# Weight splits run further ahead, adding DMAs issued earlier, the sum over the conv tiles on VectorE

## The chip, the cores and the metric

The kernel runs on one core of a Trainium2 chip. The metric is device time in microseconds (us) of one execution. PE is TensorE, DVE is VectorE, ACT is ScalarE, POOL is GpSimd, and SP is the engine whose queue issues the weight loads.

## What is computed

One layer of a decoder trunk on 256 tokens of width 1024, in float32:

```
n = RMSNorm(x)
z = n @ w_in                      # a, gate, q, k, v, qi, ki, wi, gc, ga from one projection
u = a * sigmoid(gate)
u = causal depthwise conv of u, 31 taps, per channel, + conv_b
y_conv = silu(layernorm(u) over the channels) @ w_conv_out
y_attn = attention over the 64 keys that an indexer picks, @ w_attn_out
h = x + (sigmoid(gc) * y_conv + sigmoid(ga) * y_attn) @ w_mix_out
h = h + CrossAttn(RMSNorm(h), RMSNorm(mem))       # 4 heads, 256 memory tokens
h = h + W2 relu(W1 RMSNorm(h))^2                  # 1024 -> 4096 -> 1024
return RMSNorm(h)
```

## The kernel before

**Weights.** All weights come as 83 chunks of 128x2048 float32 (1 MB each) in the order in which the products need them: conv, qi, ki, gc, ga, v, q and k, xk and xv (cross attention on the memory), ao (attention out), co (conv out), mix, xq, xo, then f1 and f2 in turn. SP loads a chunk into one of three `raw` buffers. To keep float32 precision each operand is used as a high part plus a low part, and a product takes three matmuls (high by high, high by low, low by high). So each chunk is split in two halves of 128x1024. `high()` (L185) lets ACT copy a half into a rounded `hi` tile (L189) and queues a job `low()`, which lets DVE subtract, raw - hi (L198), into a `lo` tile. For ten of the halves (the second half of every third chunk from the ninth chunk to the first of ao) it is done otherwise: ACT writes lo = -hi (L192), and `low()` has GpSimd issue a DMA that adds raw onto lo (L196). After the low of a chunk's last half, `low()` issues the load of the next chunk into the raw buffer that came free. There are six `hi` and six `lo` buffers (`HALVES`), reused in turn.

**How far ahead.** `weights()` hands a half to its user and counts it in `nused`; `nsplit` counts the halves whose high has been issued. `split_high()` issues the next high only while `nsplit - nused < HALVES - held`. `held` is 1, and is 2 where two halves are in use at once. `split_ahead()` (L230) issues one low, unless a chain has `waiting` set, and then one high. It is called once after each `weights()`.

**Order.** The order of the instructions on each engine is that in which the program issues them; the framework adds the semaphores. A tile of a result buffer that is given a new owner is written only when all instructions that use the old contents have been done. Each product goes over half chunks: `form_b` (L291) takes a half chunk, calls `split_ahead()`, runs a 128-column tile over all eight k tiles, hands the result to `after` and calls `tick()`. `form_b_late` (L302) does the same for two tiles together, with the last k tile of both left to the end, so that the operand can come late; it sets `held` to 2 for its length. It is used for the first chunk of co, mix, xq and f1 (co 0 is the first). The xo products work by k instead: `form_c` (L907) takes one half for all eight output tiles, and `form_c_last` (L917) takes both halves of the last xo chunk, and runs pairs of output tiles through both, each pair followed by `xo_residual` (L938): a DVE add into h_t, two ACT copies to the high part of `ff_p`, and one pair later two DVE instructions for its low part. f1 begins with `ff_p`.

**Fill.** The conv's 240 tap instructions on DVE (8 tiles by 30; the first tap of each tile is on ACT) are filler: `tick()` (L235) advances all pending chains by a step, and then issues taps while DVE's account stands more than 1000 below PE's. Both accounts are sums of prices in ns of what was issued on a counted engine (`pe` and `dve`, L62 to L108; a DVE instruction costs columns/0.96 plus 70, or plus 125 with a per-partition scalar). Whatever is issued through `nc.vector` or `nc.gpsimd` directly isn't counted. A finished conv tile goes into `done`; from the second on, GpSimd adds it onto `usum` (L475, 256 columns, seven times). When the eighth is finished, the chain `layer_norm` (L623) is started, before the last of these adds is issued. Its steps, one per `tick()`: one that only allocates; the mean from `usum` by a matmul (`ps_mub`) with four DVE subtractions, ACT squares and DVE adds, after which `waiting` is set until the next step, so that the next `split_ahead()` issues no low; then the variance, and the scaling and silu of four pairs of tiles into `u_p`, the operand of co. This runs during the ao products, whose results pass through DVE too (`ya`, `ga_t`, two instructions each). `gated` (L748) makes co's result into `mix_p`: ACT copies half of the bank to `yc`, DVE adds the other half, multiplies by the gate and adds (`gc_t`), ACT makes the high part of `mix_p`, and DVE the low part of the tile before.

Of the kernel before, what the change touches and what calls it, by code (L numbers as in the profile page):

```python
# [8 lines left out]
F32 = mybir.dt.float32  # L9
# [3 lines left out]
ALU = mybir.AluOpType  # L13
# [98 lines left out]
def block_kernel(ctx, tc, x, xt, mem, memt, wst, wki, vecs, convw, gout, out):  # L112
    nc = tc.nc
    ctx.enter_context(tc.manual_schedule())
    pe = Counted(nc.tensor, pe_price)
    dve = Counted(nc.vector, dve_price)
# [11 lines left out]
    def t8(name, dt=F32, shape=(P, KT, S)):  # L128
        return big.tile(list(shape), dt, tag="t8", bufs=12, name=name)
# [31 lines left out]
    def load(parts=1):  # L161
        if nload[0] >= len(STREAM):
            return
        c = nload[0]
        nload[0] += 1
        key = STREAM[c]
        raw = t8(f"raw{c}", F32, (P, N_CHUNK)) if c in EARLY else raws.tile([P, N_CHUNK], F32, tag="raw", name=f"raw{c}")
        n = KT * NK if key[0] == "ki" else N_CHUNK
        src = wki if key[0] == "ki" else wst[INDEX[key]]
        for q in range(parts):  # L170
            ns = slice(q * n // parts, (q + 1) * n // parts)
            nc.sync.dma_start(raw[:, ns], src[:, ns])
        if key in WHOLE:
            whole[key] = raw.rearrange("p (k n) -> p k n", k=2 * KT)
            return
        parts = 1 if key[0] == "ki" else 2
        for q in range(parts):
            ns = slice(q * n // parts, (q + 1) * n // parts)
            high_jobs.append(lambda ns=ns, q=q, last=q == parts - 1: high(key, c, raw, ns, q, last))

    def low_by_dma(key, c, q):

        return q == 1 and c % 3 == 2 and 8 <= c < STREAM.index(("ao", 1))

    def high(key, c, raw, ns, q, last):  # L185
        n = ns.stop - ns.start
        hi = highs.tile([P, N_CHUNK // 2], F32R, tag="hi", name=f"hi{c}_{q}")[:, :n]
        lo = lows.tile([P, N_CHUNK // 2], F32R, tag="lo", name=f"lo{c}_{q}")[:, :n]
        act(hi, raw[:, ns], AF.Copy)  # L189
        by_dma = low_by_dma(key, c, q)  # L190
        if by_dma:
            act(lo, hi.bitcast(F32), AF.Copy, scale=-1.0)  # L192

        def low():
            if by_dma:
                nc.gpsimd.dma_start(lo.bitcast(F32), raw[:, ns], accum_op=ALU.add)  # L196
            else:
                dve.tensor_tensor(out=lo, in0=raw[:, ns], in1=hi.bitcast(F32), op=ALU.subtract)  # L198
            prepared[(*key, q)] = (hi, lo)
            if last and c not in EARLY:  # L200
                load()

        low_jobs.append(low)

    def split_high():
        if high_jobs and nsplit[0] - nused[0] < HALVES - held[0]:
            nsplit[0] += 1
            high_jobs.pop(0)()

    def split_low():  # L210
        if low_jobs:
            low_jobs.pop(0)()

    nsplit, nused, held = [0], [0], [1]

    def weights(kind, i, half, kt):

        key = (kind, i, half)
        while key not in prepared:
            split_high()  # L220
            split_low()
        nused[0] += 1
        return [w.rearrange("p (k n) -> p k n", k=kt) for w in prepared.pop(key)]


    chains, fill, turn, done = [], [], [0], []
# [3 lines left out]
    def split_ahead():  # L230
        if not waiting[0]:
            split_low()
        split_high()

    def tick():  # L235
        for c in list(chains):
            if next(c, "end") == "end":
                chains.remove(c)
        while (len(fill) > 1 or (fill and (len(done) > 5 or nused[0] < 5))) and dve.total < pe.total - 1000:
            fill_one()  # L240
        dve.total = max(dve.total, pe.total - 2000)
# [14 lines left out]
    def start(gen):  # L256
        chains.append(gen)
        return gen
# [10 lines left out]
    def mm_b(ps, wh, wl, x2, kt, start, stop):  # L269
        mm3(ps, wh, wl, x2.high(kt), x2.low(kt), start, stop)  # L270
# [20 lines left out]
    def form_b(kind, i, x2, after, ps_of=ps_mm):  # L291

        for ct in range(2):
            w = weights(kind, i, ct, KT)
            split_ahead()
            ps = ps_of(f"ps_{kind}{i}{ct}")
            wide = is_wide(kind, 2 * i + ct)
            tile_b(ps, w, x2, wide=wide)
            after(2 * i + ct, ps if wide else ps[:, :S])
            tick()  # L300
# [158 lines left out]
    acc = t8("acc")  # L459
    usum = cst.tile([P, S], F32, tag="sums", bufs=2, name="usum")  # L460

    def tap(t, s):
        def go():
            j = TAPS - 1 - s
            if s == 0:
                act(acc[:, t, :], u[:, t, :], AF.Identity, scale=cw[:, t, j : j + 1], bias=cvb[:, t : t + 1])
            else:
                dve.scalar_tensor_tensor(out=acc[:, t, s:], in0=u[:, t, : S - s], scalar=cw[:, t, j : j + 1],
                                         in1=acc[:, t, s:], op0=ALU.mult, op1=ALU.add)
            if s == TAPS - 1:  # L470
                done.append(t)
                if len(done) == KT:
                    norms.append(start(layer_norm()))
                if len(done) > 1:
                    nc.gpsimd.tensor_tensor(out=usum, in0=usum if len(done) > 2 else acc[:, done[0], :],  # L475
                                            in1=acc[:, t, :], op=ALU.add)
        return go

    def conv_tile(i, half):
        key = ("conv", i)  # L480
        w = weights("conv", i, half, KT) if key not in WHOLE else None
        split_ahead()
        ps = ps_mm(f"ps_conv{i}{half}")
        if w:
            tile_b(ps, w, n2)
        else:
            for kt in range(KT):
                pe.matmul(ps[:, :S], whole[key][:, half * KT + kt, :], n_f[:, kt, :], start=kt == 0, stop=kt == KT - 1)
        return ps
# [132 lines left out]
    def layer_norm():  # L622
        u2.append(parts_t8("u_p"))  # L623
        yield
        mub = ps_aux("ps_mub")[:, :S]
        pe.matmul(mub, onesd, usum, start=True, stop=True)
        mub = mub.unsqueeze(1).to_broadcast([P, 2, S])
        vs = w2("vs", F32, (P, 2, S))
        pairs = [slice(2 * c, 2 * c + 2) for c in range(4)]
        for c, cs in enumerate(pairs):  # L630
            dve.tensor_tensor(out=acc[:, cs, :], in0=acc[:, cs, :], in1=mub, op=ALU.subtract)
            sq = vs if c == 0 else w2(f"sq_vr{c}", F32, (P, 2, S))
            act(sq, acc[:, cs, :], AF.Square)
            if c > 1:
                dve.tensor_tensor(out=vs, in0=vs, in1=before, op=ALU.add)
            before = sq
        waiting[0] = True
        yield
        waiting[0] = False
        dve.tensor_tensor(out=vs, in0=vs, in1=before, op=ALU.add)  # L640
        dve.tensor_tensor(out=vs[:, 0, :], in0=vs[:, 0, :], in1=vs[:, 1, :], op=ALU.add)
        yield
        rs = rsqrt(vs[:, 0, :], "vr")
        yield
        while len(headed) < NH:
            yield
        act(table, table, AF.Silu)
        rsb = spread(rs, "rsb").unsqueeze(1).to_broadcast([P, 2, S])
        for c in range(5):
            if c < 4:  # L650
                dve.tensor_tensor(out=acc[:, pairs[c], :], in0=acc[:, pairs[c], :], in1=rsb, op=ALU.mult)
                for t in (2 * c, 2 * c + 1):
                    act(acc[:, t, :], acc[:, t, :], AF.Silu, scale=lng[:, t : t + 1], bias=lnb[:, t : t + 1])
            if c > 0:
                parts_of(2 * c - 2)
            yield
# [260 lines left out]

    def form_c_last(kind, i, dst, x2, ks, after):
        w = [weights(kind, i, k, 1) for k in range(2)]
        held[0] = 2  # L920
        for ct in range(0, KT, 2):
            for k in range(2):
                for t in (ct, ct + 1):
                    cs = slice(t * P, t * P + P)
                    mm_b(dst[t], w[k][0][:, 0, cs], w[k][1][:, 0, cs], x2, ks + k, False, k == 1 and t % 2 == 1)
            after(ct)
            if ct % 4 == 2:
                tick()
        held[0] = 1
# [8 lines left out]
    def xo_residual(ct):  # L938
# [12 lines left out]
        lows_of.append(low)  # L951

    form_c_last("xo", 1, dst, ox2, 2, xo_residual)
    lows_of.pop()()

# [196 lines left out]
```

## Time and profile before

| | us |
|---|---|
| median of 3 runs (lowest, highest) | 516.12 (515.67, 516.19) |
| the profiled execution | 516.69 |
| its span, from the first to the last instruction | 514.9 |
| outside of the span | 1.8 |

The granted TensorE clock of the profiled execution is 0.998 of full speed over the span. The whole working below is made against the profiled execution. In the views a row gives the start in us, the length in us, the engine, the line, the operation, output<-input with the tiles' names, and in brackets the idle time of the engine ahead of it and who ended it. Instructions issued through the two counted engines all carry line 77, so they are told apart by the tiles' names.

### The profile page before, as it was taken

Reading aid. Unit: us, or ns where it says so; the run is one execution under the profiler, and the core shown is the slowest. Engines: PE = TensorE matmul, PEld = TensorE weight load, DVE = VectorE, ACT = ScalarE, POOL = GpSimd, SP = SyncE. Lnnn points to the kernel's source line nnn. Section 1 sums busy time; section 2 is a strip of 40 time slices with the busy share of each in tenths; the row PEclk is TensorE's granted clock in tenths of the full one; section 3 lists DMA queues with packets and bytes.
Section 4 is the critical chain, followed back from the end, with each engine's and each line's share of the span. In section 5 each row is a group of like instructions: output and inputs, shape, how many; then the busy total and the mean of one; then the engine's idle time right before and its main releaser. Section 6 shows DMA issues by size and latency. Waiting matters only on the chain.

```text
span 514.9 us, 8076 instructions
## 1 busy us (share of the span) xinstructions
PE 503.6 (98%) x3098; PEld 448.6 (87%) x3098; DVE 421.6 (82%) x822; ACT 305.3 (59%) x523; POOL 27.8 (5%) x40
## 2 busy tenths in 40 slices
PE   8999999999999999999999999999999999999995
PEld 6999998888899999888788998988888888888884
DVE  4998999999988999999989976796766566666565
ACT  5667666677556766748557657565644454544442
POOL 2001011101021000030000000000000000000000
PEclk9999999999999999999999999999999999999999
DMA  8946555766964644464646442546445554455402
GB/s 306 367 180 237 167 169 197 253 205 204 286 241 129 204 165 129 168 188 172 241 169 240 169 164 87 200 166 243 164 174 224 215 204 163 165 176 215 182 0 81
DMA packets 15750, 97.97 MB, mean 190 GB/s; under 512 B 1744, under 2 KB 2640, under 8 KB 5216
## 3 DMA queue, kind: packets, MB, share of 16 engines
q1 hardware_dynamic: 13952, 91.85, 48.7%
q0 software_dynamic: 1472, 5.28, 5.3%
q8 instruction: 24, 0.39, 0.3%
q10 hardware_dynamic: 288, 0.33, 0.2%
q14 instruction: 14, 0.11, 0.1%
HBM read 91.16 MB, written 1.05 MB: 179 GB/s over the span
## 4 chain that ended last, share of the span: by engine, by line
PE 74%; issue 10%; DVE 9%; DMA 4%; ACT 1%; POOL 1%; SPq 0%; POOLq 0%; DVEq 0%; ACTq 0%
PE ps_f L77 17%; PE ps_ff L77 16%; PE ps_k L77 4%; PE ps_q L77 4%; PE ps_mix L77 4%; PE ps_ga L77 4%; PE ps_v L77 4%; PE ps_co L77 4%; PE ps_conv L77 3%; DVE acc L77 3%; DVE lo L77 3%; PE ps_xo L77 3%; DMA raw<-in_wst_dram 2%; PE ps_xq L77 2%; PE ps_qi L77 2%
## 5 line engine op out<-in xcount | busy, mean ns | idle before, releaser
L77 DVE TENSOR_TENSOR lo<-raw,hi 128x1024 fp32r<-128x1024 f32 x153 | 184.9, 1220 | 3.7 <-ACT hi L189 2.2
L189 ACT ACTIVATE hi<-raw 128x1024 fp32r<-128x1024 f32 x163 | 168.6, 1047 | 5.2 <-DMA raw<-in_wst_dram 3.7
L77 DVE SCALAR_TENSOR_TENSOR acc<-u,cw,acc 128x235 f32<-128x235 f32 (+22 forms) x240 | 99.9, 472 | 0.5
L77 PE MATMUL ps_f<-ff_p,hi 128*128 128x512 f32 x256 | 89.9, 396 | 0.0
L77 PE MATMUL ps_ff<-hi,fs 128*128 128x512 f32 (+1 forms) x256 | 80.8, 387 | 0.0
L77 PE MATMUL ps_f<-ff_p,lo 128*128 128x256 f32 x256 | 66.2, 279 | 0.0
L77 PEld LDWEIGHTS ps_ff<-hi,fs 128*128 128x128 f32 x256 | 47.9, 188 | 9.2
L77 PEld LDWEIGHTS ps_f<-ff_p,hi 128*128 128x128 f32 x256 | 46.8, 188 | 9.2
L983 ACT ACTIVATE ft<-ps_f 128x256 f32<-128x256 f32 x32 | 12.2, 382 | 66.9 <-PE ps_f L77 66.9
L77 DVE TENSOR_TENSOR ft<-ps_f,ft 128x256 f32<-128x256 f32 x32 | 13.6, 424 | 45.8 <-ACT ft L983 45.8
L77 PEld LDWEIGHTS ps_f<-ff_p,lo 128*128 128x128 f32 x256 | 48.3, 189 | 2.6
L77 PE MATMUL ps_ff<-lo,fs 128*128 128x512 f32 (+1 forms) x128 | 49.4, 386 | 0.0
L77 PE MATMUL ps_conv<-n_p,hi 128*128 128x256 f32 x224 | 40.9, 285 | 0.4 <-ACT sg L494 0.4
L77 PEld LDWEIGHTS ps_conv<-n_p,hi 128*128 128x128 f32 x224 | 34.8, 191 | 1.6 <-ACT sg L494 0.8
L77 PE MATMUL ps_conv<-n_p,lo 128*128 128x256 f32 x112 | 31.7, 283 | 0.0
L77 PEld LDWEIGHTS ps_ff<-lo,fs 128*128 128x128 f32 x128 | 24.1, 188 | 4.9
L77 PE MATMUL ps_q<-n_p,hi 128*128 128x256 f32 x128 | 24.4, 291 | 0.0
L77 PE MATMUL ps_k<-n_p,hi 128*128 128x256 f32 x128 | 23.4, 284 | 0.0
L77 PE MATMUL ps_ao<-o_p,hi 128*128 128x512 f32 x64 | 22.8, 402 | 0.0
L77 PE MATMUL ps_co<-u_p,hi 128*128 128x512 f32 (+1 forms) x80 | 22.3, 351 | 0.3 <-DVE u_p L77 0.3
L77 PE MATMUL ps_mix<-mix_p,hi 128*128 128x512 f32 (+1 forms) x80 | 22.2, 351 | 0.0
L77 PE MATMUL ps_gc<-n_p,hi 128*128 128x512 f32 x64 | 22.0, 396 | 0.0
(238 smaller groups left out, 1008.5 us busy)
## 6 DMA issues: line engine op xcount, KB each, us to landing
raw<-in_wst_dram SPq DMA_DIRECT2D x80, 1024.0 KB, 4.9
lo<-raw POOLq DMA_DIRECT2D x10, 512.0 KB, 5.8
raw<-in_wst_dram SPq DMA_DIRECT2D x4, 512.0 KB, 8.9
x_rm<-in_x_dram SPq DMA_DIRECT2D x2, 512.0 KB, 3.8
mem_rm<-in_mem_dram SPq DMA_DIRECT2D x1, 1024.0 KB, 8.4
mem_t<-in_memt_dram SPq DMA_DIRECT2D x1, 1024.0 KB, 10.3
h_t<-in_xt_dram SPq DMA_DIRECT2D x1, 1024.0 KB, 7.0
out_dram<-hg SPq DMA_DIRECT2D x4, 176.0 KB, 2.1
```

The lines of the kernel that those rows point to most:

```text
L77: return fn(*args, **kwargs)
L189: act(hi, raw[:, ns], AF.Copy)
L983: act(t, ps[:, S:], AF.Copy)
```

## The change

Four edits. (1) The adding DMA of the ten halves is issued in `high()`, right after ACT's lo = -hi, and no longer in `low()`, which keeps the load of the next chunk. (2) `split_ahead()` issues a second high, once more than five halves were used, if the bound in `split_high()` lets it. (3) The seven adds onto `usum` are issued on the counted DVE, not on GpSimd. (4) `form_c_last` calls `split_ahead()` twice after it has taken its two halves, and before it sets `held` to 2.

```
         by_dma = low_by_dma(key, c, q)
         if by_dma:
             act(lo, hi.bitcast(F32), AF.Copy, scale=-1.0)
+            nc.gpsimd.dma_start(lo.bitcast(F32), raw[:, ns], accum_op=ALU.add)
 
         def low():
-            if by_dma:
-                nc.gpsimd.dma_start(lo.bitcast(F32), raw[:, ns], accum_op=ALU.add)
-            else:
+            if not by_dma:
                 dve.tensor_tensor(out=lo, in0=raw[:, ns], in1=hi.bitcast(F32), op=ALU.subtract)
...
         if not waiting[0]:
             split_low()
         split_high()
+        if nused[0] > 5:
+            split_high()
...
                 if len(done) > 1:
-                    nc.gpsimd.tensor_tensor(out=usum, in0=usum if len(done) > 2 else acc[:, done[0], :],
+                    dve.tensor_tensor(out=usum, in0=usum if len(done) > 2 else acc[:, done[0], :],
                                             in1=acc[:, t, :], op=ALU.add)
...
     def form_c_last(kind, i, dst, x2, ks, after):
         w = [weights(kind, i, k, 1) for k in range(2)]
+        split_ahead()
+        split_ahead()
         held[0] = 2
```

## Rows read from the trace of the kernel before

**Rows 1.** The page: busy time, share of the span and instructions of each engine, and further down the shares of the chain that ended last.

```profile
PE 503.6 (98%) x3098; PEld 448.6 (87%) x3098; DVE 421.6 (82%) x822; ACT 305.3 (59%) x523; POOL 27.8 (5%) x40
...
PE 74%; issue 10%; DVE 9%; DMA 4%; ACT 1%; POOL 1%; SPq 0%; POOLq 0%; DVEq 0%; ACTq 0%
```

**Rows 2.** The waits of all engines: engine and what waited <- what ended the wait: us in total, times, longest us. Those of TensorE's weight load (PEld) on which the argument rests.

```profile
PEld ps_co L77 <- DVE u_p L77: 1.4, 2, 0.9
PEld ps_xo L77 <- ACT xptr L879: 1.4, 2, 1.2
...
PEld ps_mix L77 <- DVE lo L77: 0.6, 2, 0.3
PEld ps_mub L77 <- POOL usum L475: 0.6, 1, 0.6
PEld ps_gc L77 <- DMA lo<-raw: 0.5, 1, 0.5
```

**Rows 3.** Two stretches: the end of the attention with ao, and co. The columns: the stretch, its length, busy us (instructions) of PE, PEld, DVE, ACT and POOL, the granted clock, the DMA engines' share, GB/s.

```profile
203.20:252.00 48.80, 47.68 (x265) 40.58 (x263) 48.01 (x92) 33.99 (x59) 5.57 (x5) 1.00 0.48 164
252.00:276.00 24.00, 23.98 (x149) 21.20 (x150) 21.77 (x41) 10.89 (x21) 0.00 (x0) 1.00 0.56 217
```

**Rows 4.** The chain that ended last: start, us, what. Around the first gc products, the last two links ahead of co with its own, and the first and one later f1 product (16 instructions are one wide tile).

```profile
88.28 7.78 DMA lo<-raw
96.11 2.83 PE ps_gc L77 x15
...
251.27 0.70 DVE u_p L77
252.02 20.74 PE ps_co L77 x131
...
329.31 16.83 PE ps_f L77 x96
...
365.00 5.59 PE ps_f L77 x32
```

**Rows 5.** GpSimd in time: three of the seven adds onto usum (the third row is two).

```profile
189.13 0.84 POOL L475 TENSOR_TENSOR usum<-usum,acc 128x256 f32<-128x256 f32 x1 [12.24 <-DVE acc L77]
...
222.19 0.83 POOL L475 TENSOR_TENSOR usum<-usum,acc 128x256 f32<-128x256 f32 x1 [0.77 <-DVE acc L77]
...
225.89 1.57 POOL L475 TENSOR_TENSOR usum<-usum,acc 128x256 f32<-128x256 f32 x1 [1.87 <-DVE acc L77]
```

**Rows 6.** DVE in time, from 188 to 252: two runs of six taps (acc<-u,cw,acc), the two instructions on an ao result, and a low.

```profile
188.53 2.87 DVE L77 SCALAR_TENSOR_TENSOR acc<-u,cw,acc 128x226 f32<-128x226 f32 x6
...
217.38 2.30 DVE L77 SCALAR_TENSOR_TENSOR acc<-u,cw,acc 128x236 f32<-128x236 f32 x6
...
248.89 0.42 DVE L77 TENSOR_TENSOR ya<-ps_ao,ya 128x256 f32<-128x256 f32 x1
249.34 0.43 DVE L77 TENSOR_TENSOR ga_t<-ya,ga_t 128x256 f32<-128x256 f32 x1
249.68 1.22 DVE L77 TENSOR_TENSOR lo<-raw,hi 128x1024 fp32r<-128x1024 f32 x1
```

**Rows 7.** PE in time: the matmul with usum, the last wait for u_p, and the wait of mix.

```profile
227.52 0.70 PE L77 MATMUL ps_mub<-usum,onesd 128*128 128x256 f32 x2 [0.24 <-POOL usum L475]
...
252.02 0.73 PE L77 MATMUL ps_co<-u_p,hi 128*128 128x512 f32 x2 [0.34 <-DVE u_p L77]
...
275.18 0.50 PE L77 MATMUL ps_mix<-mix_p,lo 128*128 128x256 f32 x2
```

**Rows 8.** ACT in time during co: the copy of a bank's half (yc), the high part of mix_p, a weight half's high, and the next yc.

```profile
257.46 0.36 ACT L321 ACTIVATE yc<-ps_co 128x256 f32<-128x256 f32 x1
...
259.23 0.42 ACT L755 ACTIVATE mix_p<-gc_t 128x256 fp32r<-128x256 f32 x1 [1.41 <-DVE gc_t L77]
259.55 1.05 ACT L189 ACTIVATE hi<-raw 128x1024 fp32r<-128x1024 f32 x1
260.50 0.36 ACT L321 ACTIVATE yc<-ps_co 128x256 f32<-128x256 f32 x1
```

**Rows 9.** DVE in time during co: the first instruction on each of two tiles' results, one after the other.

```profile
260.90 0.42 DVE L77 TENSOR_TENSOR yc<-ps_co,yc 128x256 f32<-128x256 f32 x1 [0.23 <-ACT yc L321]
...
263.95 0.42 DVE L77 TENSOR_TENSOR yc<-ps_co,yc 128x256 f32<-128x256 f32 x1 [0.23 <-ACT yc L321]
```

**Rows 10.** ACT in time around the last xo products: the first two and the last two of the eight high parts of ff_p.

```profile
325.75 0.91 ACT L942 ACTIVATE ff_p<-h_t,vec 128x256 fp32r<-128x256 f32 x2 [2.14 <-DVE h_t L77]
...
330.07 0.91 ACT L942 ACTIVATE ff_p<-h_t,vec 128x256 fp32r<-128x256 f32 x2 [0.53 <-DVE h_t L77]
```

**Rows 11.** DVE in time around the last xo products: the first add into h_t, the first low parts of ff_p, the last ones, and the next two weight lows.

```profile
325.03 0.69 DVE L77 TENSOR_TENSOR h_t<-ps_xo,h_t 128x512 f32<-128x512 f32 x1 [0.95 <-PE ps_xo L77]
...
327.07 0.87 DVE L77 SCALAR_TENSOR_TENSOR ff_p<-h_t,vec,ff_p 128x256 fp32r<-128x256 f32 x2
...
329.95 1.66 DVE L77 SCALAR_TENSOR_TENSOR ff_p<-h_t,vec,ff_p 128x256 fp32r<-128x256 f32 x4
331.53 2.35 DVE L77 TENSOR_TENSOR lo<-raw,hi 128x1024 fp32r<-128x1024 f32 x2
```

**Rows 12.** PE in time: the first f1 matmul, right behind the last of xo, and the first of f1's second tile.

```profile
329.15 0.40 PE L77 MATMUL ps_f<-ff_p,hi 128*128 128x512 f32 x1
...
331.38 0.64 PE L77 MATMUL ps_f<-ff_p,hi 128*128 128x512 f32 x2
```

More of the change, by code (lines that the diff above doesn't have):

```diff
@@ L192, in high @@
             act(lo, hi.bitcast(F32), AF.Copy, scale=-1.0)
+            nc.gpsimd.dma_start(lo.bitcast(F32), raw[:, ns], accum_op=ALU.add)
         def low():
-            if by_dma:
-                nc.gpsimd.dma_start(lo.bitcast(F32), raw[:, ns], accum_op=ALU.add)
-            else:
+            if not by_dma:
                 dve.tensor_tensor(out=lo, in0=raw[:, ns], in1=hi.bitcast(F32), op=ALU.subtract)
@@ L233, in split_ahead @@
         split_high()
+        if nused[0] > 5:
+            split_high()
     def tick():
@@ L474, in go @@
                 if len(done) > 1:
-                    nc.gpsimd.tensor_tensor(out=usum, in0=usum if len(done) > 2 else acc[:, done[0], :],
+                    dve.tensor_tensor(out=usum, in0=usum if len(done) > 2 else acc[:, done[0], :],
                                             in1=acc[:, t, :], op=ALU.add)
@@ L919, in form_c_last @@
         w = [weights(kind, i, k, 1) for k in range(2)]
+        split_ahead()
+        split_ahead()
         held[0] = 2
```

## The prediction
> **What bounds the kernel now.** I read first the page's engine shares and the shares of the chain [rows 1]. TensorE is busy for 98% of the span, and three quarters of the chain are its matmuls; at a granted clock of 0.998 nothing is to be won from the clock. So I read next who makes TensorE wait [rows 2]. Co waits for DVE's u_p (1.4 us with the weight loads), xo for ACT (1.4), mix for a low part (0.6), the matmul with usum for GpSimd (0.6), gc for an adding DMA (0.5). These are waits of the weight load, which runs ahead of the matmul, so the loss is smaller than their sum. All of it, xo's ACT latency included, is about 3.5 us, and that is the most that could be won: 0.7%. Then I asked what is behind TensorE at each edit. Between 203 and 252 DVE is busy 48.01 of 48.80 us [rows 3], and the chain leaves TensorE there: co starts when the last u_p is written (251.27 + 0.70, co at 252.02) [rows 4]. In this stretch every microsecond on DVE is one of the end. During co DVE is still busy 21.77 of 24.00 us [rows 3]. In ff the chain is TensorE alone, a wide tile each 2.79 us (two in 5.59) [rows 4].
>
> **The change part by part.**
>
> *The adding DMAs, earlier.* The one of them that TensorE waits for lands at 96.06, 7.78 us after its start, and gc goes on at 96.11 [rows 4]; the wait is 0.5 at the weight load, some 0.25 at the matmuls. Issued a low's turn earlier this goes: -0.25. GpSimd has no other work to hold up then: it is busy 27.8 us in all [rows 1].
>
> *The adds onto usum, on DVE.* An add of this shape and kind costs DVE 0.34 (ga_t starts at 249.34, the next at 249.68) [rows 6]: 7 x 0.34 = 2.4. In return DVE loses a disturbance. Six taps with an add of GpSimd beside them (189.13, 0.84 long [rows 5]) took 2.87, six others 2.30 [rows 6]: 0.57 by this pair. Not every add falls on a tap so fully; I take 0.4 each, 2.7 in all, so a net of -0.3 over the kernel, and for the three adds after 203 1.0 paid and 1.1 given back. The bounds for these three are 0 and 2.4 (all of 0.83 and 1.57 [rows 5]) given back.
>
> The Trainium skill ("SBUF — State Buffer", Who interferes with whom) says that a DVE instruction with two inputs in SBUF and a GpSimd instruction that reads SBUF exclude each other, and that the later one is blocked for the whole instruction. The rows here show 0.57 of 0.84; by the rule the three adds would give back the whole 2.4, and the next term would fall from 1.5 to about 0.2.
>
> *What the adds do to the order: term A.* They are now on the account that fills DVE. I added up the code's prices in the order of issue up to the third quarter of xv, after whose tick the last taps are issued before: PE's account stands at 196,720 and DVE's at 194,880, so that 196,720 - 1,000 - 194,880 = 840 is left. Seven adds are priced 256/0.96 + 70 = 337 each, 2,357 in all. So 1,517 no longer fits, which is the last add and three taps of some 0.37 us [rows 6]. They go to the next tick, layer_norm starts one tick later, and its mean stands behind the second ao tile instead of the first. The DVE-bound stretch then pays: three taps more after 203 (1.1), three adds (1.0) less 1.1 of disturbance, one more pair of ya and ga_t ahead of the last u_p (0.45 + 0.34 = 0.8 [rows 6]), less 0.25 of an earlier start by the gc wait. The sum is +1.5: u_p at 253.5, and TensorE has nothing else there. The wait of the usum matmul (0.6 at its weight load, 0.24 at the matmul) [rows 2, 7] goes, but lies inside this stretch and is worth nothing by itself. Bounds: 0.3 if the disturbance is the longest, 2.3 if nothing is given back and a tap takes longer. If the step didn't slip, 0.8 would be left of it.
>
> *A second high per step: term B.* Before, the highs run four halves ahead; now five. In most stages this moves ACT's 1.05 us by one step and costs nothing: ACT is busy for 59% of the span [rows 1] and TensorE is covered by the lead itself. A high issued earlier may wait for its raw load, and on ACT everything stands behind it: of the stages before the attention I take this at nothing, bounded by 0 and 1.5, since the banks and the lows in hand cover a step. Co is the exception. There ACT and DVE form a closed loop: ACT copies yc, DVE adds (it waits 0.23 for that copy), multiplies and adds the gate, ACT waits 1.41 for it and makes mix_p, then a high of 1.05, then the next yc [rows 8]. One round is 263.95 - 260.90 = 3.05 us [rows 9], slower than the 2.79 of TensorE's tile. `held` is 2 in the first two tiles of co, so a high is held back there and the next step issues two. The second one sits in the loop: +0.95 (259.55 to 260.50 [rows 8]) once. The lows lead by only two halves then, because layer_norm's slipped step takes one low away later than before, and TensorE already waits for lows and for mix_p's low at the start of mix, 0.6 at the weight loads [rows 2, 7]. Nothing is left to cover it: +1.0, bounds 0 and 1.1.
>
> *The two calls in form_c_last: term C.* When xo's last chunk has been taken, both its halves are in use and three more highs stand ready: five of six buffers. The first new call has `held` at 1, so its two split_highs run to five ahead: 2 + 5 = 7 tiles in six buffers. The seventh high must wait until the first half of xo's last chunk has been read for the last time. That is six matmuls before the end of xo, about 0.7 us ahead of f1's first matmul at 329.15 [rows 12], so at about 328.5. Meanwhile ACT stands, and behind that high stand all eight copies into ff_p, the first of which ran at 325.75 [rows 10]. The high takes 1.05 [rows 8], so the first ff_p copy comes at 329.7, 3.9 late. From there the loop of ACT and DVE runs on its own. ACT makes two copies in 0.9 us [rows 10]; DVE has h_t 0.6 and two lows 0.8 (four in 1.66) per pair of tiles [rows 11], in order, each pair's lows behind the next h_t. The first lows begin at 330.55, and three more rounds of about 1.4 follow with the last h_t to ff_p copies between them: the low part of k tile 6 at about 334.4. f1's first tile needs it for the seventh of its eight steps, which it now does by 331.38 [rows 12]. With the last step it is ready at 334.6 instead of 331.7: +2.85. Bounds: 0 if the seventh tile doesn't come about (an account of buffers that I have one off), 3.2 if the two weight lows that the calls also issue ahead of the h_t adds (2.35 as they ran before [rows 11], here in DVE's idle time up to 325.03) push h_t back as well. By themselves these two lows cost +0.25 to 0.4, as DVE had 0.95 idle ahead of that h_t.
>
> *In ff* the highs are five ahead instead of three. TensorE waits nowhere there, and its tiles come at 2.79 [rows 4]: no change.
>
> Sum: A 1.5 + B 1.0 + C 2.85 = 5.35, the -0.25 being in A. The profiled execution is 516.69 = 514.9 of span + 1.8; it becomes 522.0, span 520.3. That execution lies 0.57 over the median of 516.12, so for the median I forecast 521.5.
>
> **The rivals.**
>
> *Faster.* The adds fall out of GpSimd, DVE gets back more than it pays, the last taps still fit into the same tick, and C doesn't fire. Then the gc wait (0.25) goes and of co's wait for u_p some 0.9; the usum wait is inside that. 516.12 - 1.15 = 515.0. It decides at the account: if what is left before that tick were 2,357 or more instead of 840. Against it speak the prices, which are the code's own; for it, that 1,517 is three taps in 240.
>
> *C without effect.* The buffers are taken one less than I count, or ACT gets its slot in time. A + B with the lows' 0.3: 518.8.
>
> *C with only one of A and B.* The step doesn't slip, or the loop in co has slack that the records don't show: about 520. The skill's port rule gives the same: with A at 0.2, 520.2.
>
> *It doesn't do what it says.* The bound in split_high lets the lead grow by one half at most, and where ACT or a raw load is late, not at all. If the highs can't get ahead, B and C go, and A's gains and costs cancel: 516.1 to 516.9.
>
> *More.* Highs that now wait for their raw load block ACT in the stages before the attention as well, +1.5: 523 to 525.
>
> **How the numbers follow.** Forecast (A, B and C) 0.48, own range 520.3 to 522.8. C with one of A and B 0.17 (of this the port rule 0.05). C without effect 0.11. More 0.06. No change 0.09. Faster 0.09. The predicted time is that of the first. The range leaves out 2 in 10: the no-change and the faster case below, 0.18, and the upper part of the last. So it runs from 517.6 to 523.2. A measurement can tell some 0.2%, 1.0 us, from no change: faster is below 515.1, slower above 517.15. Faster 0.09, same 0.09, slower 0.82.
>
> **What would show it.** Adds: a DVE row usum of about 0.34 a piece, and no run of taps stretched beside GpSimd. Early DMA: no wait of gc for lo<-raw. A: the matmul with usum behind the second ao tile, and co's wait for u_p at about 3. B: a wait of TensorE for a low inside co or at mix, about 1 larger than now. C: a high on ACT, in the last xo product, that waits for PE ps_xo, and ps_f waiting near 3 us for ff_p. If ACT's high at xo doesn't wait for PE, C is wrong, and with it more than half of the forecast; if co starts by 252, A is wrong.

## The result and the profile after

The changed kernel takes 523.58 us (522.89 to 524.20, 4 runs) beside 516.11 of the kernel before: a ratio of 1.0146, 95% interval 1.0129 to 1.0164. It is slower, as forecast, but by 7.5 us instead of 5.4, and 0.4 beyond the upper end of the range. The profiled execution took 523.23 with a span of 521.4 and a granted clock of 0.994 (0.998 before).

The page's engine line, which answers to the first of [rows 1]. DVE is busy 420.0 us instead of 421.6 although it has seven instructions more; TensorE is busy 2.4 us more with the same 3098 matmuls.

```profile
PE 506.0 (97%) x3098; PEld 449.4 (86%) x3098; DVE 420.0 (81%) x829; ACT 306.6 (59%) x523; POOL 18.4 (4%) x33
```

Where the time went, by the start of the first matmul of each stage in the two profiled executions (co 4 is the first matmul of co's fourth tile):

| us | before | after | after less before | added since the row above |
|---|---|---|---|---|
| gc | 76.05 | 75.54 | -0.51 | -0.51 |
| ao | 224.29 | 223.54 | -0.75 | -0.24 |
| co 4 | 258.30 | 260.67 | +2.37 | +3.12 |
| mix | 272.60 | 275.92 | +3.32 | +0.95 |
| f1 | 329.15 | 334.03 | +4.88 | +1.56 |
| f2 | 345.98 | 352.22 | +6.24 | +1.36 |

From f2 on nothing is added: its last products start 6.25 later. So there are three places where time is lost, those of the terms A, B and C, and each has its rows. They add 3.12 + 0.95 + 2.92 = 6.99. Of the 0.75 gained up to ao no run shows how much is the change's: in the five profiled kernels without the first edit ao starts anywhere from 223.27 to 224.29.

The waits of all engines after (what waited <- what ended it: us, times, longest), answering to [rows 2]. The waits for usum and for an adding DMA at gc are not among them any more; that for a low at mix is unchanged (0.6), and one for a low inside co has come to it (1.0); co's wait for u_p doubled; ACT waits 4.0 us for TensorE at xo, and f1 for ff_p. ACT's highs now wait 38.0 us for their raw loads, in 15 places.

```profile
ACT hi L189 <- DMA raw<-in_wst_dram: 38.0, 15, 5.7
...
ACT hi L189 <- PE ps_xo L77: 4.0, 1, 4.0
...
PEld ps_co L77 <- DVE u_p L77: 2.9, 4, 1.3
...
PE ps_f L77 <- DVE ff_p L77: 2.0, 3, 1.4
...
PE ps_co L77 <- DVE u_p L77: 1.7, 3, 1.0
...
PEld ps_co L77 <- DVE lo L77: 1.0, 2, 0.9
...
PEld ps_mix L77 <- DVE lo L77: 0.6, 2, 0.3
```

**At co (A).** DVE after, in time: three taps and then the last usum add stand behind a low of the next step, and layer_norm's first subtraction follows at 230.17.

```profile
224.95 1.22 DVE L77 TENSOR_TENSOR lo<-raw,hi 128x1024 fp32r<-128x1024 f32 x1
226.09 1.44 DVE L77 SCALAR_TENSOR_TENSOR acc<-u,cw,acc 128x228 f32<-128x228 f32 x3
227.56 0.42 DVE L77 TENSOR_TENSOR usum<-usum,acc 128x256 f32<-128x256 f32 x1
...
230.17 1.88 DVE L77 TENSOR_TENSOR acc<-acc,ps_mub 128x512 f32<-128x512 f32 x3
```

TensorE after, in time. The matmul with usum starts 5.59 behind the first ao matmul, which is two tiles of 2.79; before it was one tile and the wait [rows 7]. In co's first tile TensorE then stands three times, 1.02, 0.34 and 0.29, and the rows behind are long: two matmuls of 512 columns in 1.22, where [rows 7] has 0.73.

```profile
229.13 0.59 PE L77 MATMUL ps_mub<-usum,onesd 128*128 128x256 f32 x2
...
250.58 0.39 PE L77 MATMUL ps_co<-u_p,lo 128*128 128x256 f32 x1 [1.02 <-DVE u_p L77]
251.31 0.50 PE L77 MATMUL ps_co<-u_p,hi 128*128 128x512 f32 x1 [0.34 <-DVE u_p L77]
...
252.44 0.58 PE L77 MATMUL ps_co<-u_p,lo 128*128 128x256 f32 x1 [0.29 <-DVE u_p L77]
253.16 1.22 PE L77 MATMUL ps_co<-u_p,hi 128*128 128x512 f32 x2
```

Busy time by stretch after (the columns of [rows 3]; the third number from the end is the granted clock). TensorE works 2.40 of the 4.20 us ahead of 253.2. The granted clock is at the lower of its two levels, 1.2 GHz, from 252.4 to 255.9 (0.51, the second row). In the 2.8 us from 253.2 on, in which TensorE is busy throughout, it is 0.52: they did the work of 2.8 x 0.52 = 1.46, so 1.34 us are lost there, with TensorE shown as busy. In the last stretch, with f1's waits, the clock stays at 1.00.

```profile
249.00:253.20 4.20, 2.40 (x9) 1.19 (x8) 4.10 (x9) 2.31 (x4) 0.00 (x0) 0.91 0.53 199
252.40:255.90 3.50, 3.32 (x10) 2.65 (x11) 3.45 (x5) 0.13 (x1) 0.00 (x0) 0.51 1.01 428
253.20:256.00 2.80, 2.80 (x9) 2.41 (x10) 2.77 (x4) 0.00 (x0) 0.00 (x0) 0.52 1.00 421
256.00:260.00 4.00, 4.00 (x25) 3.45 (x24) 1.45 (x4) 0.87 (x3) 0.00 (x0) 1.00 0.68 238
...
327.50:337.00 9.50, 7.50 (x51) 6.55 (x52) 7.00 (x13) 4.67 (x10) 0.00 (x0) 1.00 0.76 290
```

**Inside co (B).** ACT, DVE and TensorE after, one row each. Two highs in a row stand ahead of yc; DVE waits 1.18 for it instead of 0.23 [rows 9]; and two tiles on TensorE waits for a low.

```profile
261.94 1.99 ACT L189 ACTIVATE hi<-raw 128x1024 fp32r<-128x1024 f32 x2
```

```profile
264.23 0.42 DVE L77 TENSOR_TENSOR yc<-ps_co,yc 128x256 f32<-128x256 f32 x1 [1.18 <-ACT yc L322]
```

```profile
267.10 0.50 PE L77 MATMUL ps_co<-u_p,lo 128*128 128x256 f32 x2 [0.44 <-DVE lo L77]
```

**At xo (C).** ACT after, in time, answering to [rows 10]: a high waits 3.99 us until TensorE has read the first half of xo's last chunk, and the copies into ff_p begin at 332.88, behind the last matmul of xo, where before they began 3.4 ahead of f1's first [rows 10, 12].

```profile
331.91 1.06 ACT L189 ACTIVATE hi<-raw 128x1024 fp32r<-128x1024 f32 x1 [3.99 <-PE ps_xo L77]
332.88 1.69 ACT L945 ACTIVATE ff_p<-h_t,vec 128x256 fp32r<-128x256 f32 x4
```

TensorE after, in time: f1 waits for ff_p three times. Its loss by the table is 1.56 + 1.36 = 2.92.

```profile
334.03 0.47 PE L77 MATMUL ps_f<-ff_p,hi 128*128 128x512 f32 x1 [1.37 <-DVE ff_p L77]
...
335.33 0.50 PE L77 MATMUL ps_f<-ff_p,hi 128*128 128x512 f32 x1 [0.24 <-DVE ff_p L77]
...
336.73 0.50 PE L77 MATMUL ps_f<-ff_p,hi 128*128 128x512 f32 x1 [0.38 <-DVE ff_p L77]
```

### The profile page after: what moved, and what is told of

Read it like the earlier page. It is cut to its first block, busy times and chain, and to the rows that moved or that the text cites. A ratio compares the mean times of both kernels' runs of the same rounds, so it can differ in the third digit from the quotient of the medians.

```text
span 521.4 us, 8029 instructions
## 1 busy us (share of the span) xinstructions
PE 506.0 (97%) x3098; PEld 449.4 (86%) x3098; DVE 420.0 (81%) x829; ACT 306.6 (59%) x523; POOL 18.4 (4%) x33
## 4 chain that ended last, share of the span: by engine, by line
PE 83%; DVE 12%; ACT 2%; issue 2%; DMA 1%; POOL 0%; POOLq 0%; DVEq 0%; ACTq 0%
PE ps_f L77 17%; PE ps_ff L77 16%; PE ps_conv L77 9%; PE ps_k L77 4%; PE ps_q L77 4%; PE ps_mix L77 4%; PE ps_ga L77 4%; PE ps_gc L77 4%; PE ps_v L77 4%; DVE acc L77 3%; DVE lo L77 3%; PE ps_co L77 3%; PE ps_xo L77 2%; PE ps_xq L77 2%; PE ps_qi L77 2%
## 5 line engine op out<-in xcount | busy, mean ns | idle before, releaser
L189 ACT ACTIVATE hi<-raw 128x1024 fp32r<-128x1024 f32 x163 | 170.6, 1052 | 72.5 <-DMA raw<-in_wst_dram 38.0
L77 DVE SCALAR_TENSOR_TENSOR acc<-u,cw,acc 128x235 f32<-128x235 f32 (+22 forms) x240 | 98.0, 463 | 0.5
L77 PE MATMUL ps_co<-u_p,hi 128*128 128x512 f32 (+1 forms) x80 | 23.6, 365 | 0.5 <-DVE u_p L77 0.3
L77 PE MATMUL ps_ga<-n_p,hi 128*128 128x512 f32 x64 | 22.0, 396 | 0.0
```

What stands on the lines that cost most here:

```text
L77: return fn(*args, **kwargs)
```

## The experiments

The theory with which they began: A, B and C as forecast, and as a fourth term the clock, which falls because TensorE stood at co. The rivals to it: the clock fell for another reason (the weight loads, or waits of the second highs), or one of the three terms is a different mechanism that happens to cost as much. Each time stands beside that of the kernel before on the same chip.

### Without the calls in form_c_last

```
         w = [weights(kind, i, k, 1) for k in range(2)]
-        split_ahead()
-        split_ahead()
         held[0] = 2
```

> The change without its fourth edit: form_c_last no longer calls split_ahead. Theory (term C, a seventh high for six buffers blocks ACT at xo): the wait of ACT's hi for PE ps_xo (4.0 us) and the waits of ps_f for ff_p (2.0 at the matmuls) go, and the time falls by 2.9 from 523.6 to 520.7. Rival (ACT's wait only covers time that f1's start would lose anyway, for the two lows moved ahead of h_t): it falls by under 1, to 522.6 or more.

519.53 (518.65 to 520.59) beside 516.74: 1.0058, interval 1.0043 to 1.0073. From mix to f2 it takes 73.31 instead of 76.30, so C is 2.99, and ACT's wait for ps_xo is gone. The time fell by more than C: it is 2.79 over the kernel before, where the changed kernel is 7.47 over it. Four of its six executions have a granted clock of 0.997 or 0.998 and take 518.65 to 519.76; two have 0.994 and take 520.38 and 520.59. So part of the fall seems to be that the clock doesn't drop at co in every execution of this kernel; of the changed kernel's four, three have 0.994 and one 0.989. The profiled execution, at 520.38, has the drop in its rows; of the others only the mean over the span is known.

### The adds on DVE alone

```
-                    nc.gpsimd.tensor_tensor(out=usum, ...
+                    dve.tensor_tensor(out=usum, ...
```

> The kernel before with the third edit alone: the seven adds onto usum on the counted DVE. Theory (term A plus the clock): layer_norm starts one tick later, TensorE waits for u_p about 1 us longer than before, and the granted clock then falls to half for some 3 us of co, which costs another 1.3: 517.9 to 518.6. Rival 1 (the clock falls for another reason, such as the waits that the second highs add): the clock stays at 1.00 and only the longer wait is left, 516.9 to 517.4. Rival 2 (DVE gets back what it pays): 516.1.

518.86 (517.91 to 520.05) beside 516.74: 1.0047, interval 1.0032 to 1.0063. The theory holds and rival 1 falls: without any second high the clock is 0.55 in the stretch behind the wait (columns as above).

```profile
248.50:253.20 4.70, 3.00 (x14) 1.95 (x12) 4.56 (x10) 3.42 (x7) 0.00 (x0) 1.00 0.40 119
253.20:257.00 3.80, 3.49 (x12) 2.84 (x13) 3.53 (x5) 0.87 (x1) 0.00 (x0) 0.55 0.96 405
```

Here too it seems to be part of the executions: two at 0.995 (the profiled one is the slower) take 519.58 and 520.05, four at 0.998 take 517.91 to 519.29. If these four are without the drop, A by itself puts them 1.2 to 2.6 over the kernel before.

### Two highs alone

```
         split_high()
+        if nused[0] > 5:
+            split_high()
```

> The kernel before with the second edit alone: a second high per step. Theory (term B): two highs of ACT in a row in the loop of co's results, TensorE waits near the end of co for a low or for mix: 516.8 to 517.1, and the clock stays at 1.00. Rival 1 (the wait in co needs layer_norm's slipped step as well): 516.1. Rival 2 (the highs issued ahead of their raw loads block ACT elsewhere too): over 517.3.

517.24 (516.32 to 517.64) beside 516.74: 1.0010, interval 1.0001 to 1.0019. That is 0.5 over the kernel before, less than the 0.7 to 1.0 expected, and the profiled execution shows no drop of the clock at co. From co 4 to mix it takes 15.25, the same as in the changed kernel and 0.95 more than before (14.30): B is there without layer_norm's slip, and rival 1 falls. Rival 2 falls too: gc to ao takes 147.86, before 148.24. The wait, out of the waits of all engines:

```profile
PEld ps_co L77 <- DVE lo L77: 1.0, 2, 0.9
```

### The waits at co filled

```
...
+            if kind == "co" and ct == 0:
+                idle = ps_aux("ps_idle")
+                for start, end, n in ((0, 4, 5), (4, 6, 2), (6, 7, 0)):
+                    tile_b(banks[ct], ws[ct], x2, range(start, end), wide)
+                    for j in range(n):
+                        nc.tensor.matmul(idle, zero_r[:, :P], zero_r, start=True, stop=True)
...
```

> The whole change, with seven matmuls of 512 columns on a zero tile, into a bank that nobody reads, in the places of co's first tile where TensorE waits for u_p (five ahead of its fifth k tile, two ahead of its seventh): no wait is shortened, but TensorE works in most of it. Theory (the clock falls because TensorE stood in this wait): the granted clock of the stretch behind it stays at 1.00 instead of 0.52, and 1.3 us come back: 522.3. Rival (the matmuls there are slow for the weight loads that come at 421 GB/s in that stretch, or for waits before): the clock and the time stay, 523.6 or a few tenths more.

522.04 (521.64 to 522.42) beside 516.74, where the changed kernel had 523.58: 1.0109, interval 1.0095 to 1.0122. TensorE in time, and by stretch: five matmuls of nothing stand where TensorE stood for 1.02, the next co matmul is no earlier relative to ao than in the changed kernel (250.39 - 223.35 = 27.04, and 250.58 - 223.54 = 27.04), and behind it the clock is 1.00 while the weight loads run at 317 GB/s.

```profile
249.19 1.33 PE L317 MATMUL ps_idle<-zero_r 128*128 128x512 f32 x5
250.39 0.39 PE L77 MATMUL ps_co<-u_p,lo 128*128 128x256 f32 x1
```

```profile
248.50:253.20 4.70, 4.02 (x18) 2.75 (x17) 4.60 (x9) 2.62 (x5) 0.00 (x0) 1.00 0.50 192
253.20:257.00 3.80, 3.80 (x23) 3.29 (x23) 3.00 (x5) 0.38 (x1) 0.00 (x0) 1.00 0.75 317
```

The rival falls. From ao to co 4 this kernel takes 35.92, the changed one 37.13, the one before 34.01: of the 3.12 there, 1.21 is the clock and 1.91 is A. By the medians 1.5 comes back, or 2.2 if each kernel is counted from the kernel before beside it (5.30 and 7.47 over). That the low clock costs this is shown. That the waits bring it about is supported, but one rival is left, chance: all four executions here have 0.996 to 0.998, all four of the changed kernel 0.994 or less, yet the two kernels above, which ran on the chip of this one with their waits left empty, have 0.997 or more in four of six executions each.

### The adds on DVE, outside of the account

```
-                    nc.gpsimd.tensor_tensor(out=usum, ...
+                    nc.vector.tensor_tensor(out=usum, ...
```

> The kernel before with the seven adds onto usum on DVE but outside of the account (nc.vector), and nothing else. Theory (term A is the account's: three taps and the last add pushed into the next tick): layer_norm starts in the same tick as before, the wait for u_p stays within 0.5 us of before, the clock stays at 1.00, and the time within 0.6 of the kernel before. Rival (the adds' own time on DVE is what delays u_p): 1.0 or more above the kernel before, as the counted adds alone gave 2.1.

516.73 (516.38 to 517.57) beside 515.97: 1.0014, interval 1.0005 to 1.0023. The matmul with usum starts 2.82 behind ao's first (226.09 - 223.27), one tile, and ao to co 4 takes 34.36, 0.35 more than before. So of A's 1.91, 0.35 is the adds' own time and some 1.55 the step by which the account pushed layer_norm back. Counted from gc on, the step is as large (to co 4 it takes 183.79 in the kernel with the filled waits and 182.23 here), while nothing is left for the adds (182.25 in the kernel before): the account's part is shown, the adds' own is 0 to 0.35. The median is 0.76 over the kernel before, a little more than the 0.6 of the theory and less than the rival's 1.0; these rows don't show the rest.

```profile
226.09 0.59 PE L77 MATMUL ps_mub<-usum,onesd 128*128 128x256 f32 x2
```

### The calls behind held = 2

```
         w = [weights(kind, i, k, 1) for k in range(2)]
+        held[0] = 2
         split_ahead()
         split_ahead()
-        held[0] = 2
```

> The whole change with the two calls of split_ahead in form_c_last moved behind held = 2, so that no seventh high is issued for six buffers; the two weight lows still go ahead of the h_t adds. Theory (the seventh tile is all of term C): ACT's hi doesn't wait for PE ps_xo, the waits of ps_f go, and the time is that of the change without the calls, 2.8 above the kernel before, within 0.4. Rival (the lows ahead of h_t cost too): 0.4 to 1.0 more than that.

520.71 (520.41 to 521.13) beside 515.97: 1.0089, interval 1.0076 to 1.0102. ACT's wait for ps_xo is gone. From mix to f2 it takes 73.69: 2.61 less than after, 0.38 more than without the calls. So the seventh tile is 2.6 of C, and the lows ahead of h_t are some 0.3 to 0.4, as the rival had it. The time is farther over the kernel before than expected (4.7 instead of 2.8), and all four executions have a clock of 0.993 or 0.994. The two of the kernel without the calls at 0.994 are 3.75 over the kernel before on their chip, so 1.0 is left beside them, of which the rows show the 0.38. Why the clock drops in each execution of one kernel and in a third of those of the other isn't settled.

### All three terms taken out

```
-                    dve.tensor_tensor(out=usum, ...
+                    nc.vector.tensor_tensor(out=usum, ...
...
-    def split_ahead():
+    def split_ahead(more=True):
...
-        if nused[0] > 5:
+        if more and nused[0] > 5:
...
             w = weights(kind, i, ct, KT)
-            split_ahead()
+            split_ahead(kind != "co")
...
         w = [weights(kind, i, k, 1) for k in range(2)]
-        split_ahead()
-        split_ahead()
         held[0] = 2
```

The fourth part stands in form_b; form_b_late has the same.

> The whole change with each of the three terms taken out: no calls in form_c_last, no second high during co (it is kept in all other stages), and the adds onto usum on DVE but outside of the account. Theory (A with its clock, B and C are all that the change costs): within 0.5 of the kernel before. Rival (the second highs or the earlier adding DMAs cost elsewhere as well): 1 or more above it.

516.33 (516.11 to 517.22) beside 515.97: 1.0006, interval 0.9998 to 1.0015. The sum closes: what is left of the change, with its second highs in all other stages and its earlier DMAs, costs nothing that can be told, though ACT's highs wait 29.0 us for raw loads in it. The clock doesn't fall at co. Its mean over the span is 0.995 even so, since it is at the lower level at the end, where TensorE has no more work; so a mean of 0.995 by itself is no sign of a drop at co (columns as above).

```profile
230.00:270.00 40.00, 38.36 (x228) 33.23 (x227) 37.39 (x67) 24.38 (x43) 0.72 (x1) 1.00 0.47 181
509.70:514.50 4.80, 0.00 (x0) 0.00 (x0) 0.70 (x2) 0.54 (x1) 0.00 (x0) 0.51 0.31 109
```

### The earlier DMA alone

```
             act(lo, hi.bitcast(F32), AF.Copy, scale=-1.0)
+            nc.gpsimd.dma_start(lo.bitcast(F32), raw[:, ns], accum_op=ALU.add)
```

> The kernel before with the first edit alone. Theory of the prediction (the wait of gc for an adding DMA goes, 0.25): 0 to 0.3 below the kernel before, which is not to be told from no change. Rival (the DMAs collide with the weight loads earlier): 0.5 or more above it.

515.99 (515.65 to 516.85) beside 516.10: 0.9999, interval 0.9990 to 1.0007. No change. The wait of gc [rows 2] is gone, but it is also gone in the adds alone and in the two highs alone, which issue the DMA as before. In its place the adds alone wait 0.5 for such a DMA at ga, and so does this kernel, 0.3, in spite of the edit. So the wait comes and goes from one execution to the next.

```profile
PEld ps_ga L77 <- DMA lo<-raw: 0.3, 1, 0.3
```

### Less work on DVE ahead of co

Three kernels that go on from A: if DVE's work sets the start of co, then lows taken from DVE by adding DMAs should bring it forward.

```
-        return q == 1 and c % 3 == 2 and 8 <= c < STREAM.index(("ao", 1))
+        return q == 1 and (c % 3 == 2 and 8 <= c < STREAM.index(("ao", 1)) or key in (("ao", 1), ("ao", 2), ("ao", 3)))
```

with the first edit of the change; then with ("ao", 1) and ("ao", 3) only, and those two without the first edit.

> The kernel before with the first edit alone, and three more halves made by an adding DMA (the second halves of ao's second to fourth chunk), which takes three lows of 1.14 us from DVE in the stretch that ends in the wait for u_p and gives ACT three copies of 1.0. Theory (DVE's work in that stretch sets the start of co): the waits of co for u_p (1.3 us of TensorE's time) go, and the time is 1.0 to 1.5 below the kernel before. Rival (ACT's copies delay the silu of layer_norm, or the DMAs land late): no gain, or slower.

> The kernel before with the first edit, and two more halves made by an adding DMA (the second halves of ao's second and fourth chunk, not of its third, whose DMA landed too late for ao in the run with three). Theory (DVE's work ahead of u_p sets the start of co, and 2.3 us of lows taken away are more than the wait of 1.3): no wait of co for u_p and none of ao for an adding DMA, 1.0 to 1.5 below the kernel before. Rival (an adding DMA takes 4.5 to 8 us to land and comes late here too): as with three, no gain.

> The same two more halves by an adding DMA, without the first edit: each DMA is issued in its low's turn. Theory (the first edit's worth is that the DMA lands a step earlier): ao or co waits for lo<-raw, 0.3 to 2 above the run with the first edit. Rival (the lead covers the landing either way): the same as with it.

Three halves: 516.28 (515.83 to 518.50) beside 515.97, 1.0008, interval 0.9997 to 1.0019. The wait for u_p went, and ao waited for an adding DMA in its place. Two: 516.31 (514.65 to 518.78) beside 516.10, 1.0009, interval 0.9996 to 1.0022; the profiled execution, at 514.90, has a wait of 0.9 for such a DMA at ao's weight load, and the three slowest, with a mean clock of 0.995, take 517.69 to 518.78. Two without the first edit: 517.84 (516.43 to 518.90), 1.0029, interval 1.0017 to 1.0042. The rivals hold for the first two; the first edit is worth 1.5 in the last pair, as its theory had it. The wait in the kernel with three, out of all engines' waits:

```profile
PE ps_ao L77 <- DMA lo<-raw: 1.3, 1, 1.3
```

and in the one without the first edit, with TensorE's stretch around its end: one wait of 1.8, and the clock at 0.72 over 6 us, which is the lower level for 6 x 0.28 / 0.5 = 3.4 us of them.

```profile
PE ps_ao L77 <- DMA lo<-raw: 1.8, 1, 1.8
```

```profile
234.00:240.00 6.00, 4.45 (x18) 3.74 (x19) 2.55 (x5) 4.77 (x6) 1.61 (x2) 0.72 0.65 211
```

The DMAs of xv's halves stand ahead of the late usum adds on GpSimd, so they were tried last, with the first edit:

```
+        ... or key in (("xv", 0), ("xv", 1)))
```

> The kernel before with the first edit, and two more halves made by an adding DMA, now the second halves of the two xv chunks, whose DMAs stand on GpSimd's queue ahead of the late adds onto usum and land well before xv needs them. Theory (any 1.3 us of DVE work taken away between 203 and 250 brings co forward by 1.3, if no adding DMA is waited for): no wait of co for u_p, none of ao for an adding DMA, 1.0 to 1.5 below the kernel before. Rival (DVE's account moves as well, so that the work freed is filled with taps and u_p comes no earlier; or the DMA is late in some executions): within 0.5 of the kernel before.

515.72 (514.87 to 516.17) beside 516.27: 0.9985, interval 0.9976 to 0.9994. This is faster than both kernels, by 0.55 than the one before: less than the theory's 1.0, and just past the rival's 0.5. Co's wait for u_p is gone. The order moved as well, the other way than in A: the taps end a step earlier, and the matmul with usum stands ahead of ao's first tile, not behind it. There it waits 0.9 for GpSimd's last add, which takes part of the expected gain. How much of the gain is the order and how much the work taken from DVE isn't told apart.

```profile
PE ps_mub L77 <- POOL usum L474: 0.9, 1, 0.9
```

```profile
224.72 0.70 PE L77 MATMUL ps_mub<-usum,onesd 128*128 128x256 f32 x2 [0.85 <-POOL usum L474]
225.06 0.58 PE L77 MATMUL ps_ao<-o_p,hi 128*128 128x512 f32 x1
```

## Why the prediction was right and wrong

**The bound** was read rightly, and one sentence of it was wrong by what it left out: that "at a granted clock of 0.998 nothing is to be won from the clock". Nothing could be won, but it could be lost, and no term of the sum and no bound asked what a longer wait of TensorE does to its clock. That is the step that failed. In the profiled execution it is 1.21 by the kernel with the filled waits, 1.34 by the granted clock of the stretch. With it the sum would have been 5.35 + 1.2 to 1.3 = 6.6, and the profiled execution grew by 6.54. That these two agree so well is partly luck: the three places add 6.99, and the 0.75 gained ahead of ao stands where the forecast had -0.25. For the median the forecast would have been 522.7 to 522.8, inside the range, and still 0.8 below the 523.58 measured. That rest is how the two profiled executions stand to their medians: that of before was 0.57 above, that of after 0.35 below, where the forecast had taken 0.57 off both.

**The earlier DMAs:** no effect was shown by the edit alone, though its interval (0.5 below to 0.4 above) doesn't exclude the -0.25 either. That was read from a wait that comes and goes from one execution to the next.

**The adds:** the net of the three after 203 is between nothing and +0.35, forecast -0.1. What DVE gets back was forecast rightly, 2.7 for seven adds. In the kernel before, the longest tap takes 0.95; with the adds on DVE, outside of the account, none takes over 0.48. The first two rows are all taps of the two kernels (shortest, median and longest in ns), the others DVE before, in time.

```profile
L77 DVE SCALAR_TENSOR_TENSOR acc<-u,cw,acc x240: 435/464/951, 19.4 to 225.3; 128x231 f32<-128x231 f32 x8, 128x229 f32<-128x229 f32 x8, 128x227 f32<-128x227 f32 x8, 128x235 f32<-128x235 f32 x7
...
L77 DVE SCALAR_TENSOR_TENSOR acc<-u,cw,acc x240: 433/460/483, 18.5 to 224.7; 128x231 f32<-128x231 f32 x8, 128x229 f32<-128x229 f32 x8, 128x227 f32<-128x227 f32 x8, 128x235 f32<-128x235 f32 x7
...
122.62 0.43 DVE L77 TENSOR_TENSOR ga_t<-ps_ga,ga_t 128x256 f32<-128x256 f32 x1
...
189.28 0.95 DVE L77 SCALAR_TENSOR_TENSOR acc<-u,cw,acc 128x238 f32<-128x238 f32 x1
...
225.65 1.22 DVE L77 TENSOR_TENSOR lo<-raw,hi 128x1024 fp32r<-128x1024 f32 x1
...
226.78 1.76 DVE L77 TENSOR_TENSOR lo<-raw,hi 128x1024 fp32r<-128x1024 f32 x1
```

Each of the seven adds lengthens one instruction of DVE, six taps (to 0.61 to 0.95) and the low at 226.78 (1.76 instead of 1.22). That is 0.16 to 0.54 each, 2.7 in all (an estimate, from the lengths of neighbours of the same kind). The add at 225.89 [rows 5] starts while the low of 225.65 runs, which ends at 226.87, and is done at 227.46, 0.59 behind it; the next low is done at 228.54, 1.08 behind the add. The tap at 189.28 ends 0.26 behind the add of 189.13, which ended at 189.97. An instruction that reads one input from PSUM (the row at 122.62, beside the add of 122.41 to 123.32) isn't lengthened. This is what the rule of the Trainium skill ("SBUF — State Buffer", Who interferes with whom) says: the two exclude each other, and the later one waits. The prediction misread what follows from it. It took the whole length of the adds, 0.83 and 1.57, as DVE's loss, but part of that is the add's own wait: of the 1.57, 0.98 passed before the low had ended. DVE's loss to the three adds after 203 is 0.16 + 0.38 + 0.54 = 1.1, so that A doesn't fall to 0.2 by the rule.

**Term A:** the account was right to the instruction. The last add and three taps slipped, layer_norm with them, and the kernel outside of the account kept its step. The size was 1.91 from ao on against 1.8 ahead of the -0.25 (the adds 0.35 instead of -0.1, the slip 1.55 instead of 1.9). Its upper bound, 2.3, doesn't follow from its own terms: with nothing given back they add up to 2.65. The matmul with usum stands behind the second ao tile, as forecast; the wait for u_p is 2.9, forecast about 3.

**Term B:** 0.95, forecast 1.0; the two highs sit in the loop and the wait is for a low. The reason given for its being uncovered, that layer_norm's slip had taken a low away, wasn't needed: with the two highs alone the stage is as long. Nor was mix part of it: its row in [rows 7] has no wait of the matmul, and the 0.6 at the weight load is the same after.

**Term C:** 2.92, forecast 2.85; ACT's wait, its end, the copies and f1's waits came as worked out. The bound of 0.25 to 0.4 for the lows ahead of h_t is the 0.38 measured. **Highs that wait for raw loads** elsewhere: taken at nothing, and they cost nothing, although these waits are 38.0 us where they were 3.7.

**The rivals:** the faster one needed 2,357 left on the account and fell with A. C with a full seventh tile fired. ("C without effect" adds up to 518.9, not 518.8.) The case "more" named ACT blocked on raw loads, which happened and cost nothing; what made the time longer wasn't among the rivals.

## What to carry to other kernels

A bound on how far ahead work may run is a count of buffers, and it must count those still being read: two halves in use and five ahead is a seventh tile for six buffers, and the engine that waits for it holds up everything behind it in its queue. Where an account fills an engine, moving work onto the counted engine moves the order as well; here the order cost 1.55 us and the work 0.35 at most. The length of an instruction that shares with another engine holds its own wait too: what the other engine loses is read from that engine's rows. When a change adds to the waits of TensorE, look at the granted clock of the stretch behind them.

## What the runs showed of the hardware

After three waits in 3 us (1.02, 0.34, 0.29; TensorE busy 2.40 of 4.20 us) the granted clock was at its lower level from 252.4 to 255.9, and after one wait of 1.8 us for some 3.4 us. With two waits of 0.56 and 0.34 in the kernel before, with one of 1.3 in the kernel with three more adding DMAs, and with those of 1.37, 0.24 and 0.38 at f1, the profiled executions show it at 1.00. With matmuls on zeros in the waits it stayed at 1.00, and 1.2 us came back in the rows. The drop doesn't seem to come in each execution of a kernel: the mean clock points to 2 of 6 without the calls, and 2 of 6 with the adds alone. What tells these executions apart wasn't found.

An add of two tiles on GpSimd and a DVE instruction with two inputs from SBUF ran one after the other: the one that came later ended late by the rest of the other, and DVE lost 0.16 to 0.54 us to each of seven adds of 0.83 to 2.75.
